# A two-layer decoder trunk on one core: plain order in the down stages, a split last tile, turned tiles behind whole pairs, and TensorE in written order

## The chip, the cores and the metric

The program runs on one core of a Trainium2 chip. The metric is the device time of one execution in microseconds (us), lower is better. Engines are named as in the profile: PE is TensorE (matmuls), PEld its weight loads, DVE is VectorE, ACT is ScalarE, POOL is GpSimd, SP issues DMAs.

## The reference

The program computes a decoder trunk of two layers on 256 tokens of width 1024, all in float32. `D_FF` is 2816, a head has 64 columns.

```python
def swiglu(x, w_gate, w_up, w_down):
    return (jax.nn.silu(x @ w_gate) * (x @ w_up)) @ w_down
...
    for layer in range(DEPTH):
        if layer == N_A_LAYERS:
            shared_kv = shared_moba_kv(h, positions, kv_norm_g, w_kv, k_norm_g)
        h = h + 0.5 * swiglu(rms_norm(h, ffn1_norm_g[layer]), ffn1_w_gate[layer], ...)
        hn = rms_norm(h, mix_norm_g[layer])
        if layer < N_A_LAYERS:      # convolution beside attention over a memory
            ...
        else:                       # block attention over the shared keys and values, beside the same
            ...
        h = h + jnp.concatenate([primary, mem_out], axis=-1) @ w_o[layer]
        h = h + 0.5 * swiglu(rms_norm(h, ffn2_norm_g[layer]), ffn2_w_gate[layer], ...)
```

The shared keys and values come from one projection of 1536 columns (768 keys, 768 values). The keys are normed by head and turned by position.

## The kernel before

The residual `x` lies in on-chip memory as eight tiles of 128 features by 256 tokens. A product of float32 is made from parts in the faster format that the kernel calls F32R: a weight is split into a rounded high part `wh` (a copy on ACT) and the rest `wl` (a subtraction on DVE), an input `y` into halves 0 (high) and 1 (low). Three products are summed: high by high, high by low, low by high.

All weights stream through the chip once, in chunks of which each half holds eight tiles of 128 by 128. `half_hi` (named `hi`, `lo` in the plan) makes `wh` and `wl` for such a half, with four buffers each.

**One FFN** is the function `ffn`; it runs four times, under the names a, b, c and d. For each of 22 blocks `j` it makes a gate tile `pg` and an up tile `pu`, each from eight input tiles `k`. `mm2` multiplies one weight tile: the high part against both halves of the input in one matmul of 512 columns (the sums land in the two halves of one PSUM bank), then the low part against the high input, 256 columns, into the lower half. The two together are called a pair here. After the last `k` the two halves are added. Trace names: `ag`, `au`, `ao` for the gate, up and down products of FFN a, and so for b, c, d; `ahs` for the activations.

The **down stage** of an FFN makes eight output tiles `m`, each from 22 tiles `k` of the activations. For the first seven, even `k` use `mm2` and odd `k` use `mm2_lo_first`, which puts the low part's matmul first, so two matmuls of 256 and two of 512 columns alternate. The last tile (`m` 7) uses `mm3`: three matmuls of 256 columns into one half of the bank, so that nothing has to be added from the other half. Its end is two DVE operations: `scalar_tensor_tensor` (scale) and `tensor_tensor` (add to `x`). The next stage's input tile is then split.

**Order.** Instructions go to the engines as a scheduler of the framework places them, by its own simulated timeline. The kernel can bind an engine: while a letter stands in `state["order"]`, `in_order` puts each instruction of that engine behind the last one written (P is TensorE, V, A and G are DVE, ACT and POOL). FFN a runs unbound. From layer 0's mixing the order is "P" or "PVA"; `ffn("b", ...)` clears it after its block 3; FFN c is unbound; layer 1's mixing is written out step by step (`MIX1`, "PVAG"), and FFN d is unbound again. `behind` puts one instruction after another without a semaphore.

**Small work inside a group.** A `plan` maps (block, gate or up, `k`) to a function that runs within `mm2`, between its two matmuls: `mean` (a norm's sums by matmuls of one column), `rows` (`bcast_rows`: two transposes that spread the norm over the partitions, PSUM tag `aux`), and turns. A turn is `to_heads_T`: two transposes of a token tile into a PSUM tile and one ACT copy out of it. In FFN b both turns of the memory keys follow the `rows` transposes at (3, g, 3); in FFN c both turns of the third key block come at (2, g, 4).

**Shared keys and values.** Between FFN b and FFN c, `proj` runs three times (`kv0`, `kv1`, `kv2`): 48 matmuls of 512 columns each, into two PSUM tiles by token block (tag `mm`, four buffers). `kv0` makes key blocks `sk0` and `sk1`, `kv1` makes `sk2` and the first values, `kv2` the other values. A key block of one token tile is copied out by ACT into a token tile (`sk0t`, tag `tok`, two buffers), normed and rotated on DVE and POOL, and turned (`sk0p`, tag `aux`, two buffers, shared with `bcast_rows`). `sk0` and `sk1` are turned without a written place. The norm `rkv` is written ahead of `kv0`.

Of the kernel before, what the change touches and what calls it, by code (L numbers as in the profile page):

```python
# [9 lines left out]
F32 = mybir.dt.float32  # L10
# [65 lines left out]
e5.a e6.x lo18 e6.h hi19 e7.x e6.l e6.q e7.h lo19 e6.a e7.q e7.a e7.l  # L76
""".split()
AHEAD = 3

POOL_NORM = (1,)  # L80

# [12 lines left out]
V_FFN1, V_MIX, V_MEM, V_FFN2, V_KV = 0, 16, 32, 48, 64  # L94
# [7 lines left out]
G_MQ, G_MK, G_K, G_Q = 0, 1, 3, 4  # L102
# [7 lines left out]
def tile_kernel(ctx: ExitStack, tc: tile.TileContext, w, xT, memT, pos, vec, hg, const, spec, out):  # L110
# [4 lines left out]
    tp = ctx.enter_context(tc.tile_pool(name="tp", bufs=2))  # L115
# [7 lines left out]
    x = cp.tile([P, KD, SEQ], F32, name="x")  # L123
# [26 lines left out]
    nc.vector.memset(mhalf, -0.5)  # L150


    state = {"chunk": 0, "half": 0, "raw": None, "order": "", "last": {}, "between": None, "made": []}

    class Ordered:

# [36 lines left out]
    def mmul(*a, **k):  # L193
        return in_order("P", nc.tensor.matmul(*a, **k))  # L194
# [57 lines left out]
    def mm3(o, wt, y, k, first, last, **kw):  # L252
        h, l = wt
        i = mmul(o, h, y[:, k, 0], start=first, stop=False, **kw)
        mmul(o, h, y[:, k, 1], start=False, stop=False, **kw)
        mmul(o, l, y[:, k, 0], start=False, stop=last, **kw)
        return i

    def mm2(o, wt, y, k, first, last, turn=None):

        h, l = wt
        a = mmul(o, h, y[:, k].rearrange("p a s -> p (a s)"), start=first, stop=False)
        if turn is not None:
            state["between"] = a
            turn()
            last_turn, state["between"] = state["between"], None
        b = mmul(o[:, :SEQ], l, y[:, k, 0], start=False, stop=last)
        if turn is not None:
            behind(b, last_turn)

    def mm2_lo_first(o, wt, y, k, last):
        h, l = wt
        mmul(o[:, :SEQ], l, y[:, k, 0], start=False, stop=False)
        mmul(o, h, y[:, k].rearrange("p a s -> p (a s)"), start=False, stop=last)

    def mm_group2(o, y, turns):
        for k, wt in enumerate(tiles_of(1)):
# [10 lines left out]
    def mm3_tok(o, wh, wl, y, t, k, c, first, last):  # L288
        s = slice(t * P, (t + 1) * P)
        mmul(o, y[:, k, 0, s], wh[:, c], start=first, stop=False)  # L290
        mmul(o, y[:, k, 0, s], wl[:, c], start=False, stop=False)
        mmul(o, y[:, k, 1, s], wh[:, c], start=False, stop=last)
# [33 lines left out]
        state["stat"] = state["last"]["P"]  # L326
        return v

    def rstd_cols(name, acc):
        v = mean_cols(name, acc)  # L330
        r = tp.tile([P, NT], F32, name=name, tag="rc", bufs=3)
        gps.tensor_tensor(r, v, mhalf[:, :NT], op=ALU.pow)
        return r

# [16 lines left out]
        return tp.tile([P, SEQ], F32, name=name, tag="acc")  # L351

    def ffn(name, y, acc, nexts, store=False, quick=False, hook=None, after=None, hook_down=None, r=None, plan=None,
            early=None, turns=()):


        plan = plan or {}
# [9 lines left out]

        def rows():
            norm["rb"] = bcast_rows(name + "nb", norm["r"])
            for turn in turns:  # L370
                turn()
# [15 lines left out]
        for j in range(KF):  # L387
# [27 lines left out]
            else:  # L415
# [10 lines left out]
                else:  # L426
                    mm_group2(pg, y, planned(j, "g"))
                    mm_group2(pu, y, planned(j, "u"))
            if early and j == 3:
                state["order"] = ""  # L430
            if j == 0 and "mean" not in plan.values() and r is None:
                mean()
            if rb is None and j < rows_at[0]:
# [19 lines left out]
        for m in range(KD):  # L453
            po = psum(f"{name}o{m}")
            if hook_down:
                with tc.issue_after(state["act"].ins):
                    hook_down(m)

            both_sums = m < KD - 1
            for k in range(KF):  # L460
                if both_sums and k % 2:
                    mm2_lo_first(po, next(it), hs, k, k == KF - 1)
                elif both_sums:
                    mm2(po, next(it), hs, k, k == 0, False)
                else:
                    mm3(po[:, :SEQ], next(it), hs, k, k == 0, k == KF - 1)
            if both_sums:
                d = both_halves(f"{name}d{m}", po, "g")
                dve.scalar_tensor_tensor(d, d, 0.5, rb, op0=ALU.mult, op1=ALU.mult)
            else:  # L470
                d = tp.tile([P, SEQ], F32, name=f"{name}d{m}", tag="g")
                dve.scalar_tensor_tensor(d, po[:, :SEQ], 0.5, rb, op0=ALU.mult, op1=ALU.mult)
            dve.tensor_tensor(x[:, m], d, x[:, m], op=ALU.add)
# [45 lines left out]
    def proj(name, y, *uses):  # L519

        os_ = [psum(f"{name}{t}") for t in range(NT)]
        n = MW * len(uses)
        per = HC // n
        for k0 in range(0, KD, per):
            wh, wl = half_chunk()
            for t in range(NT):
                for i in range(per):
                    k = k0 + i
                    mm3_tok(os_[t][:, :n], wh, wl, y, t, k, slice(i * n, (i + 1) * n), k == 0, k == KD - 1)
        for t in range(NT):  # L530
            for i, use in enumerate(uses):
                use(t, os_[t][:, i * MW:(i + 1) * MW])
# [152 lines left out]
    kv0 = []  # L685
# [456 lines left out]
    def sum_squares():  # L1142
# [7 lines left out]
        for t, tt in found:  # L1150
            key1.normed(t, tt)
        state["order"] = "P"

    (ykv, y), acc = ffn("b", y, acc, (V_KV, V_FFN1 + KD), plan={(2, "u", 1): "mean", (3, "g", 3): "rows"},
                        early=sum_squares, turns=mem_turns)


    rkv = rstd_cols("rkv", acc)
    turns = []
# [471 lines left out]
```

## Time and profile before

| | us |
|---|---|
| median of 3 runs | 962.6 |
| lowest and highest run | 961.28, 963.98 |
| the profiled execution, its own time | 963.06 |
| span from its first to its last instruction | 961.3 |

The profiled execution is 0.46 us above the median, and 1.8 us of its time lie outside its span. Views used below: the page's part 1 (busy time of each engine, its share of the span, its instructions); part 4 (the chain of work that ended last, shares by engine); the waits (who waited for whom: total us, times, longest); the chain in order of time (start, length, what, how many); and the timeline (start, length, engine, line, operation, tiles, shapes, count; idle time before it and what ended that in brackets). Matmul rows last longer than their distance, because matmuls are pipelined; the text therefore goes by starts. A transpose is a PE row of 128 columns.

### The profile page before, as it was taken

Reading aid. Unit: us, or ns where it says so; the run is one execution under the profiler, and the core shown is the slowest. Engines: PE = TensorE matmul, PEld = TensorE weight load, DVE = VectorE, ACT = ScalarE, POOL = GpSimd, SP = SyncE. Lnnn points to the kernel's source line nnn. Section 1 sums busy time; section 2 is a strip of 40 time slices with the busy share of each in tenths; the row PEclk is TensorE's granted clock in tenths of the full one; section 3 lists DMA queues with packets and bytes.
Section 4 is the critical chain, followed back from the end, with each engine's and each line's share of the span. In section 5 each row is a group of like instructions: output and inputs, shape, how many; then the busy total and the mean of one; then the engine's idle time right before and its main releaser. Section 6 shows DMA issues by size and latency. Waiting matters only on the chain.

```text
span 961.3 us, 15012 instructions
## 1 busy us (share of the span) xinstructions
PE 953.0 (99%) x5670; PEld 832.1 (87%) x5670; DVE 721.9 (75%) x1263; ACT 575.1 (60%) x1057; POOL 90.0 (9%) x89
## 2 busy tenths in 40 slices
PE   8999999999999999999999999999999999999998
PEld 6888888897888888888988888888897998888887
DVE  6898777776889877767767777767779578777663
ACT  6676566556686655655556665555548666556442
POOL 0122000110012000000123000000134120000000
PEclk9999999999999999999999999999999999999999
DMA  8755455454346555555555555555552245555550
GB/s 293 289 200 188 176 194 200 176 176 152 111 137 222 187 200 175 193 201 176 185 196 189 176 184 208 179 181 205 183 177 74 103 175 182 207 181 182 208 203 21
DMA packets 26569, 174.11 MB, mean 181 GB/s; under 512 B 3329, under 2 KB 4865, under 8 KB 6145
## 3 DMA queue, kind: packets, MB, share of 16 engines
q1 hardware_dynamic: 26208, 172.99, 50.5%
q8 instruction: 44, 0.72, 0.3%
q10 hardware_dynamic: 288, 0.17, 0.1%
q14 instruction: 29, 0.23, 0.1%
HBM read 172.10 MB, written 1.05 MB: 180 GB/s over the span
## 4 chain that ended last, share of the span: by engine, by line
PE 93%; DVE 4%; DMA 1%; ACT 1%; issue 0%; POOL 0%; SPq 0%
PE cg L194 8%; PE do L194 6%; PE ao L194 6%; PE co L194 6%; PE bo L194 6%; PE bu L194 6%; PE dg L194 6%; PE cu L194 6%; PE du L194 6%; PE bg L194 6%; PE ag L194 6%; PE au L194 6%; PE kv L194 3%; PE obo L194 2%; PE mkv L194 2%; DVE room L164 2%
## 5 line engine op out<-in xcount | busy, mean ns | idle before, releaser
L164 DVE TENSOR_TENSOR wl<-raw,wh 128x1024 fp32r<-128x1024 f32 (+1 forms) x326 | 395.8, 1216 | 168.7 <-ACT wh L164 166.8
L164 ACT ACTIVATE wh<-raw 128x1024 fp32r<-128x1024 f32 (+1 forms) x326 | 341.1, 1050 | 296.1 <-PE dg L194 27.1
L194 PE MATMUL ag<-y,wh 128*128 128x512 f32 x176 | 63.7, 398 | 0.5 <-ACT wh L164 0.5
L194 PE MATMUL au<-y,wh 128*128 128x512 f32 x176 | 63.4, 396 | 0.0
L194 PE MATMUL bg<-oay,wh 128*128 128x512 f32 x176 | 62.4, 393 | 0.1
L194 PE MATMUL dg<-oby,wh 128*128 128x512 f32 x176 | 62.5, 392 | 0.0
L194 PE MATMUL cu<-by,wh 128*128 128x512 f32 x176 | 62.3, 393 | 0.0
L194 PE MATMUL du<-oby,wh 128*128 128x512 f32 x176 | 62.3, 391 | 0.0
L194 PE MATMUL cg<-by,wh 128*128 128x512 f32 x176 | 62.2, 392 | 0.0
L194 PE MATMUL bu<-oay,wh 128*128 128x512 f32 x176 | 62.2, 392 | 0.0
L194 PE MATMUL bo<-bhs,wh 128*128 128x512 f32 (+1 forms) x198 | 55.8, 368 | 0.0
L194 PE MATMUL co<-chs,wh 128*128 128x512 f32 (+1 forms) x198 | 55.8, 368 | 0.0
L194 PE MATMUL do<-dhs,wh 128*128 128x512 f32 (+1 forms) x198 | 55.8, 368 | 0.0
L194 PE MATMUL ao<-ahs,wh 128*128 128x512 f32 (+1 forms) x198 | 55.8, 368 | 0.0
L194 PE MATMUL ag<-y,wl 128*128 128x256 f32 x176 | 48.9, 280 | 2.2 <-DVE wl L164 2.2
L194 PE MATMUL cg<-by,wl 128*128 128x256 f32 x176 | 49.4, 281 | 0.0
L194 PE MATMUL bg<-oay,wl 128*128 128x256 f32 x176 | 49.4, 281 | 0.0
L194 PE MATMUL bu<-oay,wl 128*128 128x256 f32 x176 | 49.4, 281 | 0.0
L194 PE MATMUL dg<-oby,wl 128*128 128x256 f32 x176 | 49.4, 280 | 0.0
L194 PE MATMUL cu<-by,wl 128*128 128x256 f32 x176 | 49.3, 280 | 0.0
L194 PE MATMUL du<-oby,wl 128*128 128x256 f32 x176 | 49.3, 280 | 0.0
L194 PE MATMUL au<-y,wl 128*128 128x256 f32 x176 | 48.7, 279 | 0.0
(960 smaller groups left out, 2242.9 us busy)
## 6 DMA issues: line engine op xcount, KB each, us to landing
raw<-in_w SPq DMA_DIRECT2D x158, 1024.0 KB, 4.8
raw<-in_w SPq DMA_DIRECT2D x5, 512.0 KB, 10.4
mT<-in_memT SPq DMA_DIRECT2D x1, 1024.0 KB, 8.4
out<-x SPq DMA_DIRECT2D x8, 128.0 KB, 1.7
dft<-in_spec SPq DMA_DIRECT2D x1, 817.0 KB, 10.2
raw<-in_w SPq DMA_DIRECT2D x2, 256.0 KB, 3.9
x<-in_xT SPq DMA_DIRECT2D x1, 512.0 KB, 8.8
x<-in_xT SPq DMA_DIRECT2D x2, 128.0 KB, 3.2
```

The source lines that it names most:

```text
L164: i = f(*a, **k)
L194: return in_order("P", nc.tensor.matmul(*a, **k))
```

## The change

The edit has four parts.

- **Down stages.** `mm2_lo_first` goes; tiles 0 to 6 use `mm2` for every `k`. Tile 7 uses `mm2` for `k` 0 to 13 (`APART` = 14), then `mm3` for `k` 14 to 21. After `k` 13 the upper half of its bank is scaled and added to `x` (`taken(po[:, SEQ:])`, two DVE operations), and after `k` 21 the lower half in the same way.
- **Small work behind whole pairs.** `mm2` runs its turn after both matmuls; the next pair's first matmul is put behind the turn's last transpose (`held`). The memory keys' two turns move from (3, g, 3) to (3, g, 4) and (3, g, 5), those of `sk2` from (2, g, 4) to (2, g, 6) and (3, g, 4).
- **TensorE in written order.** FFN b no longer clears the order after block 3; FFNs b, c and d set it to "P" after block 2.
- **Shared keys.** All key blocks are turned at written places: token tile 0 of `sk0` and `sk1` after `kv1`, token tile 1 of both after `kv2`, just ahead of FFN c's `bcast_rows`. The norm `rkv` is computed within `kv0`, behind its third weight half.

```diff
-    def mm2(o, wt, y, k, first, last, turn=None):
+    def mm2(o, wt, y, k, first, last, turn=None, closes=False, **kw):
         h, l = wt
-        a = mmul(o, h, y[:, k].rearrange("p a s -> p (a s)"), start=first, stop=False)
+        a = mmul(o, h, y[:, k].rearrange("p a s -> p (a s)"), start=first, stop=closes, **kw)
+        if state["held"] is not None:
+            behind(a, state["held"])
+            state["held"] = None
+        b = mmul(o[:, :SEQ], l, y[:, k, 0], start=False, stop=last, **kw)
         if turn is not None:
-            state["between"] = a
+            state["between"] = b
             turn()
-            last_turn, state["between"] = state["between"], None
-        b = mmul(o[:, :SEQ], l, y[:, k, 0], start=False, stop=last)
-        if turn is not None:
-            behind(b, last_turn)
-
-    def mm2_lo_first(o, wt, y, k, last):
...
+            state["held"], state["between"] = state["between"], None
...
-            if early and j == 3:
-                state["order"] = ""
+            if j == 2 and not first:
+                state["order"] = "P"
...
+            def taken(half):
+                d = tp.tile([P, SEQ], F32, name=f"{name}d{m}", tag="g")
+                dve.scalar_tensor_tensor(d, half, 0.5, rb, op0=ALU.mult, op1=ALU.mult)
+                dve.tensor_tensor(x[:, m], d, x[:, m], op=ALU.add)
+
             for k in range(KF):
-                if both_sums and k % 2:
-                    mm2_lo_first(po, next(it), hs, k, k == KF - 1)
-                elif both_sums:
-                    mm2(po, next(it), hs, k, k == 0, False)
+                if both_sums:
+                    mm2(po, next(it), hs, k, k == 0, k == KF - 1)
+                elif k < APART:
+                    mm2(po, next(it), hs, k, k == 0, False, closes=k == APART - 1, skip_group_check=True)
                 else:
-                    mm3(po[:, :SEQ], next(it), hs, k, k == 0, k == KF - 1)
+                    mm3(po[:, :SEQ], next(it), hs, k, False, k == KF - 1, skip_group_check=True)
+                if not both_sums and k == APART - 1:
+                    taken(po[:, SEQ:])
...
     def proj(name, y, *uses, within=None):
...
+            if within is not None and k0 == KD // 2:
+                within()
...
-    kuse = [keys(f"sk{i}", rkv, G_K, kTs, 2 * i, True, turns if i == 2 else None, 1) for i in range(3)]
+    kuse = [keys(f"sk{i}", rkv, G_K, kTs, 2 * i, True, turns[i], 1) for i in range(3)]
...
-    proj("kv0", ykv, kuse[0], kuse[1])
+    proj("kv0", ykv, kuse[0], kuse[1], within=lambda: rstd_cols("rkv", acc, rkv))
     proj("kv1", ykv, kuse[2], vuse[0])
+    turns[0][0]()
+    turns[1][0]()
     proj("kv2", ykv, vuse[1], vuse[2])
+    turns[0][1]()
+    turns[1][1]()
     (y,), acc = ffn("c", y, acc, (V_MIX + KD,), after=AF.Exp, r=rkv,
-                    plan={(2, "g", 4): lambda: [turn() for turn in turns]})
+                    plan={(2, "g", 6): turns[2][0], (3, "g", 4): turns[2][1]})
```

More of the change, by code (lines that the diff above doesn't have):

```diff
@@ L78 @@
 AHEAD = 3
+APART = 14
 POOL_NORM = (1,)
@@ L150, in tile_kernel @@
     nc.vector.memset(mhalf, -0.5)
-    state = {"chunk": 0, "half": 0, "raw": None, "order": "", "last": {}, "between": None, "made": []}
+    state = {"chunk": 0, "half": 0, "raw": None, "order": "", "last": {}, "between": None, "held": None, "made": []}
     class Ordered:
@@ L257, in mm3 @@
         return i
-    def mm2(o, wt, y, k, first, last, turn=None):
+    def mm2(o, wt, y, k, first, last, turn=None, closes=False, **kw):
         h, l = wt
-        a = mmul(o, h, y[:, k].rearrange("p a s -> p (a s)"), start=first, stop=False)
+        a = mmul(o, h, y[:, k].rearrange("p a s -> p (a s)"), start=first, stop=closes, **kw)
[3 more added lines that the diff above has]
+        b = mmul(o[:, :SEQ], l, y[:, k, 0], start=False, stop=last, **kw)
         if turn is not None:
-            state["between"] = a
+            state["between"] = b
             turn()
-            last_turn, state["between"] = state["between"], None
-        b = mmul(o[:, :SEQ], l, y[:, k, 0], start=False, stop=last)
-        if turn is not None:
-            behind(b, last_turn)
-    def mm2_lo_first(o, wt, y, k, last):
-        h, l = wt
-        mmul(o[:, :SEQ], l, y[:, k, 0], start=False, stop=False)
-        mmul(o, h, y[:, k].rearrange("p a s -> p (a s)"), start=False, stop=last)
+            state["held"], state["between"] = state["between"], None
     def mm_group2(o, y, turns):
@@ L327, in mean_cols, with rstd_cols @@
         return v
-    def rstd_cols(name, acc):
+    def rstd_cols(name, acc, r=None):
         v = mean_cols(name, acc)
-        r = tp.tile([P, NT], F32, name=name, tag="rc", bufs=3)
+        if r is None:
+            r = tp.tile([P, NT], F32, name=name, tag="rc", bufs=3)
         gps.tensor_tensor(r, v, mhalf[:, :NT], op=ALU.pow)
@@ L353, in ffn @@
     def ffn(name, y, acc, nexts, store=False, quick=False, hook=None, after=None, hook_down=None, r=None, plan=None,
-            early=None, turns=()):
+            early=None):
         plan = plan or {}
@@ L369, in rows @@
             norm["rb"] = bcast_rows(name + "nb", norm["r"])
-            for turn in turns:
-                turn()
         def planned(j, which):
@@ L469, in ffn @@
                 dve.scalar_tensor_tensor(d, d, 0.5, rb, op0=ALU.mult, op1=ALU.mult)
+                dve.tensor_tensor(x[:, m], d, x[:, m], op=ALU.add)
             else:
-                d = tp.tile([P, SEQ], F32, name=f"{name}d{m}", tag="g")
-                dve.scalar_tensor_tensor(d, po[:, :SEQ], 0.5, rb, op0=ALU.mult, op1=ALU.mult)
-            dve.tensor_tensor(x[:, m], d, x[:, m], op=ALU.add)
+                taken(po[:, :SEQ])
             if store:
@@ L517, in to_heads_T, with proj @@
                              pp[:, :2 * P].rearrange("p (a b) -> p a b", a=2), AF.Copy, scale=scale)
-    def proj(name, y, *uses):
+    def proj(name, y, *uses, within=None):
         os_ = [psum(f"{name}{t}") for t in range(NT)]
@@ L1152, in sum_squares @@
         state["order"] = "P"
[L1154 to L1159, printed above, removed]
-    kuse = [keys(f"sk{i}", rkv, G_K, kTs, 2 * i, True, turns if i == 2 else None, 1) for i in range(3)]
+    (ykv, y), acc = ffn("b", y, acc, (V_KV, V_FFN1 + KD), plan={(2, "u", 1): "mean", (3, "g", 3): "rows", (3, "g", 4): lambda: mem_turns[0](),
+                              (3, "g", 5): lambda: mem_turns[1]()},
+                        early=sum_squares)
+    rkv = tp.tile([P, NT], F32, name="rkv", tag="rc", bufs=3)
+    turns = [[] for _ in range(3)]
+    kuse = [keys(f"sk{i}", rkv, G_K, kTs, 2 * i, True, turns[i], 1) for i in range(3)]
     vuse = [values(f"sv{i}", rkv, vs, i * MW) for i in range(3)]
-    proj("kv0", ykv, kuse[0], kuse[1])
+    proj("kv0", ykv, kuse[0], kuse[1], within=lambda: rstd_cols("rkv", acc, rkv))
     proj("kv1", ykv, kuse[2], vuse[0])
+    turns[0][0]()
+    turns[1][0]()
     proj("kv2", ykv, vuse[1], vuse[2])
+    turns[0][1]()
+    turns[1][1]()
     (y,), acc = ffn("c", y, acc, (V_MIX + KD,), after=AF.Exp, r=rkv,
-                    plan={(2, "g", 4): lambda: [turn() for turn in turns]})
+                    plan={(2, "g", 6): turns[2][0], (3, "g", 4): turns[2][1]})
     qT = cp.tile([P, KD, SEQ], F32, name="q1T", tag="t8k")
```

## The prediction, made before the change was run

> **What bounds the kernel now.** I read the page's part 1 first, then its part 4, then TensorE's waits.
>
> ```profile
> PE 953.0 (99%) x5670; PEld 832.1 (87%) x5670; DVE 721.9 (75%) x1263; ACT 575.1 (60%) x1057; POOL 90.0 (9%) x89
> ...
> PE 93%; DVE 4%; DMA 1%; ACT 1%; issue 0%; POOL 0%; SPq 0%
> ```
>
> ```profile
> PE ag L194 <- DVE wl L164: 2.2, 1, 2.2
> PE pw L131 <- DVE onec L133: 1.4, 1, 1.4
> PE ag L194 <- ACT wh L164: 0.5, 2, 0.3
> PE a4pp L197 <- ACT room L164: 0.2, 1, 0.2
> ```
>
> TensorE is busy for 99% of the span and carries 93% of the chain. All its waits add up to 4.3 us, and all but 0.2 us of that lies in the start-up and FFN a, which the edit leaves alone there. So there is almost nothing to win from waits: a gain can only come from denser matmuls, and any wait that the edit puts in front of TensorE is paid in full.
>
> How dense the matmuls are comes from two views. First the chain in order of time, in FFN d:
>
> ```profile
> 790.71 2.77 PE dg L194 x16
> ...
> 893.33 2.77 PE du L194 x16
> 896.10 61.53 PE do L194 x374
> ```
>
> From 790.71 to 896.10 lie 38 groups of eight pairs in plain order: 105.39/304 = 346.7 ns a pair. Second the timeline of the same FFN's down stage:
>
> ```profile
> 895.94 0.39 PE L194 MATMUL do<-dhs,wh 128*128 128x512 f32 x1
> ...
> 949.39 0.63 PE L194 MATMUL do<-dhs,wh 128*128 128x512 f32 x3
> 949.87 0.28 PE L194 MATMUL do<-dhs,wl 128*128 128x256 f32 x1
> ...
> 957.34 0.28 PE L194 MATMUL do<-dhs,wl 128*128 128x256 f32 x1
> 957.65 0.42 DVE L164 SCALAR_TENSOR_TENSOR dd<-do,dnb 128x256 f32<-128x256 f32 x1 [6.07 <-PE do L194]
> ```
>
> From 895.94 to 949.39 go 153 pairs and one low matmul, in alternating order: (53.45 − 0.12)/153 = 348.6 ns a pair. From the first to the last low matmul of tile 7, 949.87 to 957.34, go 21 triples: 355.7 ns each. DVE starts 0.31 us after the last matmul's start and takes 0.42 us; both are used below.
>
> **Part by part.** The sum is made on the profiled execution (963.06 us, 0.46 us above the median of 962.6).
>
> *Plain order in tiles 0 to 6.* No instruction is added or removed. If the pairs run as in the gate stage, 154 × (348.6 − 346.7) = 0.29 us an FFN, 1.2 us in four. If the 1.9 ns come from another thing than the order, it is 0; I see no reason for a loss. I take −1.2, because the gate rows are the same matmuls in the very order that is written now.
>
> The Trainium skill ("TensorE: Matmul & The Clock Gate", section "Back-to-back issue gap") gives an isolated matmul N/2.4 + 2.5 ns, which is 325 ns a pair and the same in either order; by it this term would be an estimate of 0 and the whole sum 1.2 us higher. The trace has 346.7 and 348.6 ns, so the rule's level does not fit here and I go by the rows.
>
> *Pairs in tile 7.* 14 triples become pairs, 14 matmuls and their weight loads fewer: 14 × (355.7 − 346.7) = 0.13 us an FFN, −0.5 us in four. The eight triples left keep their price.
>
> *The early half of tile 7.* This adds two DVE operations beside TensorE. Their own time (0.42 us each) is covered, as DVE is only 75% busy. But the first reads the upper half of a PSUM bank whose lower half the next matmul writes. What happens then is shown where layer 1's mixing does the same: there `mqJ` holds two token blocks in one bank, ACT reads the first block, and TensorE then writes the second.
>
> ```profile
> 704.50 0.28 PE L194 MATMUL mqJ<-wh,cy 128*128 128x256 f32 x1
> ...
> 704.63 0.50 PE L194 MATMUL rqp<-onec,cacc 128*128 128x1 f32 x4
> 704.83 0.39 ACT L164 ACTIVATE room<-mqJ 128x256 f32<-128x256 f32 x1 [0.33 <-PE mqJ L194]
> 705.26 0.19 PEld L194 LDWEIGHTS mqJ<-wh,cy 128*128 128x128 f32 x1 [0.22 <-ACT room L164]
> 705.26 0.38 PE L194 MATMUL mqJ<-wh,cy 128*128 128x256 f32 x1
> ...
> 705.49 0.28 PE L194 MATMUL mqJ<-wl,cy 128*128 128x256 f32 x1
> ```
>
> The read runs from 704.83 to 705.21 (columns of the first block only); the weight load for the second block is released by that read, at 705.26. So the halves of a bank are not independent: TensorE waits until the reader is done, starts 0.05 us later, and its first matmul then takes 0.23 instead of 0.12 us. In tile 7 the same matmul order is bound, with nothing to put in between (FFN a is unbound, but the mixing's first matmul stands behind FFN a's last). Everything behind `k` 13 queues behind that wait: 24 matmuls, and through them the next stage.
>
> The Trainium skill says the same from the hardware's side ("PSUM — Partial Sum Buffer", section "PSUM bank collisions raise a hardware error"): accesses of two engines to one bank collide at disjoint columns too, so software must guard by bank. It speaks against the change, and the row above agrees with it.
>
> Without other work on DVE, counted from tile 7's start S: the last low matmul before the wait starts at 14 × 0.3467 − 0.12 = 4.73, DVE at 5.04, TensorE again at 5.04 + 0.42 + 0.05 = 5.51 instead of 4.85, and 0.11 us for the slow first matmul: 0.77 us. That is FFN d, where DVE has only tile 6's end. In a, b and c the splits of tile 6 stand at that very place:
>
> ```profile
> 202.85 0.96 DVE L164 SCALAR_TENSOR_TENSOR ay<-x,vt,ay 128x256 fp32r<-128x256 f32 x1
> ```
>
> ```profile
> 478.38 1.36 DVE L164 SCALAR_TENSOR_TENSOR by<-x,vt,by 128x256 fp32r<-128x256 f32 x2
> 480.07 1.23 DVE L164 TENSOR_TENSOR wl<-raw,wh 128x1024 fp32r<-128x1024 f32 x1 [0.33 <-ACT wh L164]
> ```
>
> ```profile
> 697.01 0.96 DVE L164 SCALAR_TENSOR_TENSOR cy<-x,vt,cy 128x256 fp32r<-128x256 f32 x1
> ```
>
> Tile 7 starts 53.69 us after the stage (949.39 + 0.24 − 895.94). The stages start here:
>
> ```profile
> 144.63 0.39 PE L194 MATMUL ao<-ahs,wh 128*128 128x512 f32 x1
> ```
>
> ```profile
> 420.18 0.39 PE L194 MATMUL bo<-bhs,wh 128*128 128x512 f32 x1
> ```
>
> ```profile
> 638.80 0.39 PE L194 MATMUL co<-chs,wh 128*128 128x512 f32 x1
> ```
>
> So S is 198.32, 473.87 and 692.49. DVE comes free at S + 5.49 (a), S + 5.87 (b) and S + 5.48 (c); with 0.03 to start, 0.42, 0.05, 0.11 and less 4.85 that makes 1.25, 1.63 and 1.24 us. Sum over four: +4.9 us. Ends: four times the bare 0.77, +3.1, if DVE takes the early half first; and 1.23 us more in three FFNs, +8.6, if a weight copy like the one at 480.07 is placed ahead of it. I take 4.9, the order in which things become ready in these rows.
>
> *Transposes behind whole pairs.* The counts stay. A pair with two transposes in it:
>
> ```profile
> 786.16 0.39 PE L194 MATMUL dg<-oby,wh 128*128 128x512 f32 x1
> 786.39 0.38 PE L197 MATMUL dnbp<-cst,dnr 128*128 128x128 f32 x2
> 786.53 0.36 PE L194 MATMUL dg<-oby,wl 128*128 128x256 f32 x1
> 786.73 0.40 PE L194 MATMUL dg<-oby,wh 128*128 128x512 f32 x1
> ```
>
> It takes 0.57 instead of 0.35 us, 0.11 us a transpose, which is about the distance of two transposes; breaking the pair costs nothing beyond that. Moving them: 0. In FFN c the turns need `sk2` some 15 us after `kv2`, which is ample.
>
> *Written order.* In the trace no wait of TensorE lies in b, c, d or the key stretch, so there is nothing to win. There is one place to lose. Ahead of FFN c the written order is two transposes of `sk0`, two of `sk1`, two of `bcast_rows`: three tiles on the two buffers of `aux`, so the third must wait for ACT's copy out of the first, with FFN c's first matmul behind it. Before, the scheduler had spread them:
>
> ```profile
> 514.45 0.38 PE L197 MATMUL sk0p<-cst,sk0t 128*128 128x128 f32 x2
> ```
>
> ```profile
> 515.61 0.38 PE L197 MATMUL sk1p<-cst,sk1t 128*128 128x128 f32 x2
> ...
> 518.65 0.38 PE L197 MATMUL cnbp<-cst,rkv 128*128 128x128 f32 x2
> ```
>
> ```profile
> 514.93 0.48 ACT L164 ACTIVATE kvs<-sk0p,vt 128x256 f32<-128x256 f32 x1
> 515.29 0.48 ACT L164 ACTIVATE sk2t<-kv,rkv 128x256 f32<-128x256 f32 x1
> 515.64 1.22 ACT L164 ACTIVATE kvs<-kv,rkv 128x256 f32<-128x256 f32 x3
> ...
> 517.02 1.10 ACT L164 ACTIVATE wh<-raw 128x1024 fp32r<-128x1024 f32 x1
> 517.97 0.52 ACT L164 ACTIVATE kvs<-sk1p,vt 128x256 f32<-128x256 f32 x1
> ```
>
> From a turn to its copy went 0.48 us for one and 2.36 us for the other, since ACT was full. Adding 0.48 for the copy and 0.05, less the 0.44 us of the four transposes, TensorE would wait 0.6 to 2.4 us; I take the middle, 1.5, since here too value copies and a weight copy come due on ACT just then. Earlier, `sk0` and `sk1` of token tile 1 can only be copied out when the turns of tile 0 have freed their two token buffers, and `kv2`'s second tile waits for the PSUM that they hold: a race within a few tenths, 0 to 1.1 us (one ACT weight copy); I take 0.3. The norm inside `kv0` costs the same matmuls at another place: 0. Key stretch: +1.8, ends 0.6 and 3.5.
>
> **Sum:** −1.2 − 0.5 + 4.9 + 0 + 1.8 = +5.0 us. On the median: 967.6 us, 0.5% slower.
>
> **The rivals.**
> - *Not slower: the halves of tile 7's bank are independent.* If the matmul of `k` 14 needn't wait for the read of other columns, the 4.9 us go and the sum is +0.1: 962.7 us; with a free key stretch −1.7: 960.9. The `mqJ` rows speak against it. It decides as soon as the four waits together stay under 2.8 us (then the sum is under 0.3%).
> - *Waits at their bare size.* DVE takes the early half first (3.1) and ACT copies `sk0p` at once (0.6): −1.7 + 3.7 = +2.0, 964.6 us. Against it: DVE's splits in a, b and c are due before the early half is.
> - *A weight copy ahead of the early half* in a, b and c: +3.7 on the forecast, 971.3 us. Against it: in b the copy waits for ACT until 480.04, after the early half is due.
>
> **How the numbers follow.** Under about 0.3% (2.9 us) a measurement of this kernel can't be told from no change: 959.7 to 965.5 is "same". Forecast 0.55, weight copies ahead 0.13, bare waits 0.19, independent halves 0.10, something outside this list that helps 0.03. The forecast's own ends (plain order worth 0, key stretch 0.6 to 3.5) span 966.4 to 970.5. The range must take in bare waits and most of the weight-copy case: 963.5 to 971.5. Slower: 0.55 + 0.13 = 0.68; same 0.28; faster 0.04.
>
> **What would show it.** The waits of TensorE list `ao`, `bo`, `co`, `do` released by DVE, 0.6 to 1.6 us each; the same before `cnbp`, released by ACT. The chain has down stages whose first seven tiles take 53.4 instead of 53.7 us. The prediction is wrong if those waits are missing, if DVE's early half starts before the splits of tile 6, or if plain pairs in the down stage take other than 346.7 ns.

## The result, and the profile after

The changed kernel takes 972.82 us (median; 971.48 to 974.75) against 962.37 for the kernel before on the same chip: ratio 1.0109 [1.0083, 1.0135], 10.4 us slower. The forecast was 967.6 us, so it had the direction and a little under half of the size; the time lies above its range. The profiled execution takes 971.59 us.

The page's parts 1 and 4 of the changed kernel:

```profile
PE 956.9 (99%) x5614; PEld 832.8 (86%) x5614; DVE 726.0 (75%) x1271; ACT 575.1 (59%) x1057; POOL 88.3 (9%) x89
...
PE 91%; DVE 5%; ACT 1%; DMA 1%; issue 1%; POOL 0%; SPq 0%; ACTq 0%
```

TensorE has 56 matmuls fewer and is busy 3.9 us longer: so some of the loss is not waiting but slower matmuls. The rest is in its waits:

```profile
PE cnbp L198 <- ACT kvs L165: 2.5, 1, 2.5
...
PE bo L195 <- DVE bd L165: 1.2, 1, 1.2
PE co L195 <- DVE cd L165: 0.8, 1, 0.8
PE ao L195 <- DVE ad L165: 0.8, 1, 0.8
...
PE do L195 <- DVE dd L165: 0.6, 1, 0.6
PE kv L195 <- ACT sk1t L165: 0.4, 1, 0.4
```

These six are new and make 6.3 us. All of the kinds that the prediction named are there, the one ahead of `cnbp` longer than forecast. The chain in order of time (start, length, what, how many) tells how dense the matmuls are:

```profile
317.41 2.77 PE bu L195 x16
...
417.25 2.77 PE bu L195 x16
...
520.63 0.43 PE cnbp L198 x2
521.06 3.60 PE cg L195 x14
524.66 2.84 PE cu L195 x14
...
528.19 2.77 PE cg L195 x16
...
903.64 58.98 PE do L195 x336
...
963.22 3.09 PE do L195 x24
```

From 317.41 to 417.25 lie 36 groups of eight pairs: 346.7 ns a pair, as in the gates of before. But the down stage's 168 plain pairs take 58.98/168 = 351.1 ns, and the first groups of FFN c (3.60 us for seven pairs) are far slower than those behind them.

By stage, from the start of one to the start of the next, in us:

| | before | after | difference |
|---|---|---|---|
| down stages a, b, c, d | 61.53, 61.52, 61.52, 61.52 | 62.89, 63.29, 62.92, 62.65 | +5.66 |
| of these, tile 7 | 7.83 each | 8.84, 9.24, 8.85, 8.60 | +4.20 |
| `kv0` to the start of FFN c's gates | 34.05 | 37.66 | +3.62 |
| gates of c | 123.06 | 124.14 | +1.08 |
| everything else behind 145 us | | | −0.23 |

That is +10.1 us. The stretch up to the first down stage, in which the edit moves only the norm's few small matmuls, was 1.6 us shorter in this execution (143.0 for 144.6; it lies between 142.6 and 146.0 in all profiled executions here), so the two profiled executions differ by 8.5.

### The profile page after: what moved, and what is told of

The parts are those of the page before. It is cut to its first block, busy times and chain, and to the rows that moved or that the text cites. A ratio compares the mean times of both kernels' runs of the same rounds, so it can differ in the third digit from the quotient of the medians.

```text
span 969.8 us, 14952 instructions
## 1 busy us (share of the span) xinstructions
PE 956.9 (99%) x5614; PEld 832.8 (86%) x5614; DVE 726.0 (75%) x1271; ACT 575.1 (59%) x1057; POOL 88.3 (9%) x89
## 3 DMA queue, kind: packets, MB, share of 16 engines
HBM read 172.10 MB, written 1.05 MB: 179 GB/s over the span
## 4 chain that ended last, share of the span: by engine, by line
PE 91%; DVE 5%; ACT 1%; DMA 1%; issue 1%; POOL 0%; SPq 0%; ACTq 0%
PE cg L195 8%; PE do L195 6%; PE cu L195 6%; PE bu L195 6%; PE dg L195 6%; PE du L195 6%; PE bg L195 6%; PE co L195 6%; PE bo L195 6%; PE ao L195 6%; PE ag L195 6%; PE au L195 6%; PE kv L195 3%; PE obo L195 2%; PE mkv L195 2%; DVE room L165 2%
## 5 line engine op out<-in xcount | busy, mean ns | idle before, releaser
L195 PE MATMUL bo<-bhs,wh 128*128 128x512 f32 (+1 forms) x184 | 62.0, 384 | 1.2 <-DVE bd L165 1.2
L195 PE MATMUL co<-chs,wh 128*128 128x512 f32 (+1 forms) x184 | 62.0, 384 | 0.8 <-DVE cd L165 0.8
L195 PE MATMUL ao<-ahs,wh 128*128 128x512 f32 (+1 forms) x184 | 61.9, 384 | 0.8 <-DVE ad L165 0.8
L195 PE MATMUL do<-dhs,wh 128*128 128x512 f32 (+1 forms) x184 | 62.0, 384 | 0.6 <-DVE dd L165 0.6
L195 PE MATMUL co<-chs,wl 128*128 128x256 f32 x176 | 49.9, 283 | 0.0
L195 PE MATMUL bo<-bhs,wl 128*128 128x256 f32 x176 | 49.9, 283 | 0.0
L195 PE MATMUL do<-dhs,wl 128*128 128x256 f32 x176 | 49.9, 283 | 0.0
L195 PE MATMUL ao<-ahs,wl 128*128 128x256 f32 x176 | 49.7, 283 | 0.0
```

## The experiments

Four questions: do tile 7's waits come from the shared bank; does the key stretch wait for a PSUM buffer, and what do the slow pairs behind it come from; why do plain pairs not take 346.7 ns; and do the moved turns cost anything.

**Own bank for the end of tile 7** (from the changed kernel):

```diff
-                    mm3(po[:, :SEQ], next(it), hs, k, False, k == KF - 1, skip_group_check=True)
+                    if k == APART:
+                        rest = psum(f"{name}p{m}")
+                    mm3(rest[:, :SEQ], next(it), hs, k, k == APART, k == KF - 1)
```

Both halves of `po` are taken after `k` 13, `rest` after `k` 21.

> The changed kernel, but tile 7's last eight k go to a PSUM tile of their own, so that DVE's early read and TensorE's next matmul meet in different banks (two DVE operations more per FFN). Theory (the waits in tile 7 are the shared bank): no wait of TensorE on DVE in ao, bo, co, do; tile 7 takes 14 x 351.3 + 8 x 355.7 = 7.76 us in each FFN instead of 8.84, 9.24, 8.85 and 8.6; about 4.5 us less than the changed kernel, 968.3 us. Rival (DVE is simply late, or holds something else that the matmuls need): waits of about 1 us stay, 972 to 973 us.

Measured: 969.98 us, 1.0074 [1.0054, 1.0094]. The waits of `ao`, `bo`, `co`, `do` are gone, and tile 7 takes 7.80, 7.76, 7.80 and 7.76 us: 4.4 us less than in the changed kernel. The timeline of FFN b shows TensorE passing where it stood for 1.24 us before:

```profile
479.55 0.29 PE L195 MATMUL bo<-bhs,wl 128*128 128x256 f32 x1
...
479.68 0.40 PE L195 MATMUL bp<-bhs,wh 128*128 128x256 f32 x2
...
480.53 0.74 DVE L165 SCALAR_TENSOR_TENSOR bd<-bo,bnb 128x256 f32<-128x256 f32 x2
```

DVE reads the old bank 0.85 us after TensorE has gone on in the new one. DVE is as late as before and TensorE no longer waits, so meeting in one tile and one bank is shown to be the cause. The edit gives the end a tile and a bank of its own at once; whether the program's wait goes by the tile or by the bank, it does not tell. The time fell by only 2.8 us; in the profile FFN c's gates ran slow (125.86 us for 124.14), which is the last question.

**Own tag for the early transposes**: FFN c's `bcast_rows` takes its PSUM tile from `sc`, which is idle there, and not from `aux`.

```diff
-        pb = psum(name + "p", "aux", 2)
+        pb = psum(name + "p", "sc" if name == "cnb" else "aux", 2)
```

> The changed kernel, but FFN c's row transposes take a PSUM tile of the tag sc instead of the third of aux. Theory (the wait ahead of them is for ACT's copy out of the first of two buffers, and the half clock behind it comes from TensorE's idle time): the wait of 2.5 us goes, the granted clock stays at 1.0 through FFN c's first blocks, and 2.7 + 1.5 = 4.2 us go: 968.6 us. Rival (the clock falls there for another reason, as the load after a stretch of wide matmuls): only 2.7 us go, 970.1 us, and a stretch of about 3.4 us at half clock stays.

Measured: 971.88 us, 1.0097 [1.0075, 1.0119]. The wait ahead of `cnbp` is gone, the stretch takes 34.92 us instead of 37.66, and the first 14 pairs of FFN c run at full speed. So the wait is for the third tile on two buffers, as predicted. The time hardly moved; c's gates took 124.55 us in the profile, more than with the wait, at the slower of two paces that are told of below.

**The wait filled**: 11 matmuls on constants stand in TensorE's order between the turns and `cnbp`, so that it is busy while it would wait.

```diff
+    pf = psum("fill", "sc", 2)
+    for i in range(11):
+        mmul(pf, busy[:, :P], busy, start=True, stop=True)
     (y,), acc = ffn("c", ...
```

> The changed kernel with eleven matmuls of 512 columns in the 16-bit format, whose results nobody reads, put between the last turn and FFN c's row transposes: about 2.4 us of TensorE work inside a wait of 2.7 us. Theory (idle time halves the clock): the wait for ACT stays where it is, but TensorE is busy through it; no half clock behind it, 1.5 us less: 971.3 us. Rival (the clock falls for another reason): the half clock stays, 972.8 us or more.

Measured: 972.29 us, 1.0097 [1.0077, 1.0116]; the key stretch is as long as before the filling (37.71 us), c's gates are 122.82 instead of 124.14, while those of b, far ahead of the edit, took 125.80 instead of 123.76 in this execution and hide the gain. Windows of this kernel, of the changed one and of the one with its own tag (length, busy time and count of PE, PEld, DVE, ACT, POOL, then TensorE's granted clock, DMA share, GB/s):

```profile
518.00:520.60 2.60, 0.10 (x1) 0.00 (x0) 1.08 (x1) 2.60 (x7) 0.00 (x0) 1.00 0.44 186
520.60:523.00 2.40, 2.37 (x12) 2.05 (x13) 1.52 (x6) 1.68 (x5) 0.03 (x1) 0.79 0.37 116
523.00:526.00 3.00, 3.00 (x13) 2.62 (x12) 1.44 (x4) 0.00 (x0) 2.65 (x3) 0.60 0.63 262
```

(the changed kernel);

```profile
520.60:523.00 2.40, 2.24 (x13) 0.98 (x11) 1.23 (x1) 2.40 (x7) 0.00 (x0) 1.00 0.30 119
523.00:526.00 3.00, 3.00 (x19) 2.62 (x18) 1.37 (x5) 1.36 (x5) 0.94 (x1) 1.00 0.63 213
```

(filled);

```profile
523.00:526.00 3.00, 3.00 (x19) 2.65 (x18) 1.38 (x5) 1.85 (x5) 1.54 (x2) 1.00 0.86 314
```

(own tag). A further changed kernel, the one with `hs` at another place (below), has the same wait of 2.53 us, unfilled, ahead of `cnbp` at 524.13. Its window right behind it:

```profile
524.10:526.50 2.40, 2.37 (x14) 2.09 (x15) 1.52 (x6) 1.69 (x5) 0.02 (x1) 1.00 0.48 113
```

In the changed kernel TensorE is idle from 518.1 on, and from 521.9, 1.3 us after it has resumed, its pairs start 640 ns apart for about 3.4 us, at half the clock; 13 matmuls start in a window that elsewhere holds 19. Where the same wait is filled with work, or isn't there, the clock stays at 1.00. The mean granted clocks of the timed executions agree: 0.998 in all four of the changed kernel, 0.999 or 1.000 in all four of the filled one.

But the drop doesn't come each time. Five profiles have the wait unfilled; in four of them a stretch of 3.41 us at half clock follows, which begins between 0.2 us ahead of `cnbp` and 1.3 us behind it, and in the fifth the clock stayed at 1.00 and c's gates took 122.82 us, as with the wait filled. So idleness can lower the clock here, and when it does, the price behind a 2.5 us wait is another 1.3 us (124.14 against 122.82); what decides whether it does stays open. The Trainium skill ("TensorE: Matmul & The Clock Gate", section "What's actually happening") has a window of 3413 ns for this gate, after which an idle engine falls to half its clock; the length of the slow stretch agrees, but 2.53 us of idleness were enough here in four profiles of five.

**Alternating down tiles**: the changed kernel with `mm2_lo_first` at odd `k` of tiles 0 to 6 again.

> The changed kernel with the alternating order of before in the down stages' tiles 0 to 6. Theory (the order of the two widths sets the pair's time in this stage): a pair goes from 351.3 back to 348.5 ns, 0.43 us an FFN, 1.7 us in all: 971.1 us. Rival (something else in the changed kernel slows the pairs, such as the bound order or other DVE and ACT work beside them): 351 ns stay, 972.8 us.

**The kernel before with plain order alone**:

```diff
-                if both_sums and k % 2:
-                    mm2_lo_first(po, next(it), hs, k, k == KF - 1)
-                elif both_sums:
-                    mm2(po, next(it), hs, k, k == 0, False)
+                if both_sums:
+                    mm2(po, next(it), hs, k, k == 0, k == KF - 1)
```

> The kernel before with only the plain order in the down stages' tiles 0 to 6. Theory (the order of the widths alone): 351.0 ns a pair, +1.5 us over the kernel before, hardly measurable. Rival (the bound order or the new tile 7 slows the pairs): 346.7 to 348.6 ns, 0 to -1.2 us.

Measured: 973.06 us, 1.0099 [1.0072, 1.0126] for the first (its start took 145.6 us in its profile, 2.6 more than the changed kernel's, and c's gates 126.1); 963.34 us, 1.0015 [1.0006, 1.0024] for the second. By stage they agree with each other: the pairs of tiles 0 to 6 take 348.5 ns in alternating and 351.0 in plain order. FFN d's down stage in the chain, plain in the second, where the prediction showed 61.53 for the alternating one:

```profile
895.52 62.00 PE do L194 x374
```

**`hs` at another place**: the changed kernel, with the activations in a pool of their own at higher addresses.

```diff
-        hs = cp.tile([P, KF, 2, SEQ], F32R, name=name + "hs", tag="hs")
+        hs = hp.tile([P, KF, 2, SEQ], F32R, name=name + "hs", tag="hs")
...
```

The tiles `hc` and `room`, which share the buffer of `hs`, move with it.

> The changed kernel with the activations of the down stages moved from low addresses of the on-chip memory to high ones, above the weights and the inputs; nothing else. Theory (plain pairs take 351 instead of 346.7 ns because of where their moving operand lies): the down stages' pairs go to 346.7 ns, about 2.6 us less. Rival (place does not matter; the down stage falls into the slower of two paces that the gate stages show too, 346.7 and 353.3 ns): 351 ns stay.

Measured: 972.32 us in one execution. The down pairs are no longer 351.0 ns in all FFNs but 352.1 in a, 353.3 in b, 346.7 in c and in d. In b, c and d the gates just ahead ran at these very paces (353.3, 346.7 and 346.7). In a the gates ended at 346.7, and so the down stage began; from the 26th pair on it ran at 353.2. There, in the unbound FFN a, the matmuls of two neighbouring pairs stand in swapped order (timeline of TensorE):

```profile
152.49 0.62 PE L196 MATMUL ao<-ahs,wh 128*128 128x512 f32 x2
152.95 0.40 PE L196 MATMUL ao<-ahs,wl 128*128 128x256 f32 x2
```

The same swap with the same change of pace stands in the last kernel below. The chain of FFN d:

```profile
905.12 58.25 PE do L196 x336
```

58.25/168 = 346.7 ns, for 351.1 in the changed kernel. Only places in memory were changed, so plain order isn't slow as such: where its operands lie decides. Taking `hs` out of its pool may also move what lies above it, so that it is the place of `hs` alone is argued: the weights pass through the same buffers in the gates, and these kept their two paces.

**All three repairs together** (own bank, own tag, alternating):

> The changed kernel with all three repairs: tile 7's last eight k in a bank of their own, FFN c's row transposes on the tag sc, alternating order in tiles 0 to 6. What stays of the change are pairs in tile 7, turns behind whole pairs and the bound order. Theory (the slowdown is the shared bank 4.5, the wait with the clock behind it 4.2, the order of widths 1.6 us): within 0.1% of the kernel before, +0.3 us (-0.3 for tile 7, +0.6 for the wait in kv2 that stays). Rival (binding TensorE's order costs by itself): 2 us or more above the kernel before.

Measured: 965.34 us (962.59 to 967.57), 1.0033 [1.0023, 1.0043]. The down stages take 61.45, 61.43, 61.42 and 61.41 us, the key stretch 34.94. About 3 us over before remain. 0.9 of them are the key stretch; behind it c's gates took 124.55 us in the profile, for 123.06 before, and in the gates what is left of the change is the place of the turns and TensorE's written order.

**Where the turns stand.** The gates of b, c and d run at one of two paces, 346.7 or 353.3 ns a pair, in plain order at the same clock, and keep a pace until something interrupts the row of pairs. The profile of before shows such a change (chain, FFN b):

```profile
308.15 2.83 PE bg L194 x16
...
314.25 1.30 PE bg L194 x7
315.55 0.22 PE bnbp L197 x2
315.77 0.44 PE mk1p L197 x4
316.21 1.52 PE bg L194 x9
317.73 2.77 PE bu L194 x16
```

The groups take 2.83 us ahead of the transposes and 2.77 behind them; FFN c does the same at its turns. A second execution of the changed kernel, unchanged, was to show how much hangs on it:

> The changed kernel once more, unchanged, to see what in the traces repeats. Theory (a stretch of plain pairs settles on one of two paces by chance, at each interruption): waits in tile 7 and ahead of FFN c repeat to within 0.1 us and the down stages take 351 ns again, but one gate stage or another may run at 353.3 instead of 346.7 ns, worth about 2 us each. Rival (the pace is a property of the program): FFN b, c and d's gate stages take 346.7 ns again.

It took 975.83 us, 4.2 more than the first, with the same waits in tile 7 and ahead of `cnbp`. Its gates of b and c took 125.76 and 126.39 us instead of 123.76 and 124.14. The chain in FFN b:

```profile
317.45 2.83 PE bu L195 x16
...
419.21 2.83 PE bu L195 x16
```

36 groups in 101.76 us are 353.3 ns a pair, with the clock at 1.00. So two kernels tested the turns' place alone. First the repaired kernel with turns inside pairs again:

```diff
         a = mmul(o, h, ...)
-        if state["held"] is not None:
-            behind(a, state["held"])
-            state["held"] = None
+        if turn is not None:
+            state["between"] = a
+            turn()
+            last_turn, state["between"] = state["between"], None
         b = mmul(o[:, :SEQ], l, ...)
-        if turn is not None:
-            state["between"] = b
-            turn()
-            state["held"], state["between"] = state["between"], None
+        if turn is not None:
+            behind(b, last_turn)
```

> The kernel with all three repairs (own bank in tile 7, own tag for the early transposes, alternating down tiles), and the turned tiles again inside the pairs of the gates, so that TensorE resumes after them with a low matmul of 256 columns. Theory (the pace of the pairs holds until TensorE is interrupted, and a resumption with the low matmul sets the fast one): the gates of b and c run at 346.7 ns a pair for most of their length in every execution, as in before (123.8 and 123.1 us); the time is about 2.0 us below the 965.3 of the repaired kernel with turns behind whole pairs: 963.3, its runs within 961.5 to 964.5. Rival (the pace is set by chance at the start of a layer, and where the turns stand doesn't matter): 965.3 as before, runs spread over 962.6 to 967.6, with gates at 353.3 ns in some traces.

Then the kernel before with the opposite edit and nothing else:

> The kernel before with one part of the change alone: the turned tiles stand behind whole pairs, and TensorE resumes with the high matmul of 512 columns. Nothing else differs. Theory (such a resumption leaves a slow pace as it is): the gates of b and of c, which begin at 353.3 ns a pair in the profile of before, keep that pace in many executions, for up to 2 us each: median 963.5 to 966, with a spread of runs of 3 to 5 us. Rival of the prediction (where the turn stands costs nothing): 962, with the spread of before (961 to 964).

Measured: 962.72 us (960.64 to 966.20), 1.0006 [0.9996, 1.0016], against 1.0033 for the same kernel with turns behind whole pairs; and 963.83 us (961.07 to 967.61), 1.0019 [1.0005, 1.0032], against 1 for the same kernel with turns inside. So the place of the turns costs about 2 us in both, by the timed runs, and as the first of the two kept the written order, that order isn't what costs. Nor is it the clock: with the executions at a mean granted clock of 0.998 or less left out, the 21 of the kernel before lie at 960.95 to 962.44 us, and of the nine of its edited twin four lie at 965.70 to 966.20. The profiled executions at hand showed no difference (c slow in both of the first pair, b and c fast in both of the second), so four more were taken, of the two kernels unchanged.

> The repaired kernel with turns inside the pairs once more, unchanged (median 962.7, but 966.2 in its profiled execution, with the gates of c at 353.3 ns and 146.0 us up to the first down stage). Theory (the pace changes from execution to execution, and turns inside pairs make the fast one the more frequent): an execution of 961 to 963 with c at 346.7 ns, some 122.6 us for its gates. Rival (c is always slow with the early transposes on their own tag): c at 124.5 us again, the difference in the start alone.

> The repaired kernel with turns inside pairs a third time, unchanged. Theory: the gates of c at 122.6 us in an execution of 961 to 963. Rival: 124.5 us.

> The kernel before with turns behind whole pairs once more, unchanged (median 963.8, runs 961.1 to 967.6; its profiled execution of 962.1 had b and c fast). Theory: in executions of 963.5 and more b or c (or both) at 353.3 ns, 125.4 and 125.0 us for their gates instead of 123.8 and 123.1. Rival (the spread is the start's alone): b and c as in before, 143 to 146 us up to the first down stage.

> The kernel before with turns behind whole pairs a third time, unchanged. Theory: b or c at 353.3 ns where the execution takes 963.5 us or more. Rival: the start alone differs.

The first two took 965.62 and 966.11 us, both with c at 124.56 us and a late start (145.4 and 145.9): here the rival was right, and no profile of this kernel shows c fast. The late starts have a cause of their own in part: between 10 and 17 us the mean granted clock is 0.76 in both, as in four other profiles here (first down stage at 144.8 to 146.0 us in these six), and 1.00 in the fourteen others (142.6 to 145.6). That its runs of 960.6 to 961.7 had c fast is argued from their time alone: its profiled executions, with their starts put at 143 us, would come to about 963.2. The other two took 967.15 and 962.14 us. The chain of the slower one in FFN b:

```profile
317.94 2.82 PE bu L194 x16
...
419.70 2.82 PE bu L194 x16
```

and of the first execution of this kernel (962.14 us as well):

```profile
316.97 2.77 PE bu L194 x16
...
416.81 2.77 PE bu L194 x16
```

101.76 against 99.84 us for 36 groups; c went with it (125.08 against 123.06 us). Together 3.9 of the 5.0 us between the two, the rest is the start (144.9 against 143.9). So behind whole pairs the slow pace can hold through both stages, as the theory says, in one profile of three; the three kernels that are before but for the down stages and have the turns inside (before itself, plain order alone, and the last one below) have b and c at the fast pace behind the turns in their profiles, one each. With turns inside and c slow in three profiles of the repaired kernel, the traces alone don't tell the two places apart; the timed runs do.

My theory also had a rule for it: that a resumption with the matmul of 256 columns sets the fast pace. It was put to a direct test, with many cuts by two transposes of a constant, in a repeating order of one inside a pair (resumed with 256 columns) and two ahead of a pair (512):

> The repaired kernel with turns inside pairs, and two further transposes of a constant in nearly every group of eight pairs of the gates of b, c and d (from the fourth tile on), by turns inside a pair, so that TensorE resumes with the low matmul of 256 columns, and twice ahead of a pair, so that it resumes with the high one of 512. The time is longer by these transposes and is not compared; what counts is the pace of the pairs ahead of and behind each of some 110 cuts. Theory (a resumption with the low matmul sets the fast pace, one with the high matmul may leave or bring the slow one): behind a low resumption 346.7 ns nearly always, whatever stood ahead; slow stretches begin only behind high resumptions and last over the next of them. Rival (each interruption draws the pace anew by chance): slow stretches as often behind the one as behind the other. Second rival (the pace hangs on the layer's operands): whole layers at one pace, whatever the cuts.

Measured: 988.1 us, and the opposite. Behind the cuts inside a pair (with the few of the kernel's own) 35 of 38 fast stretches went slow (353.8 ns), behind those ahead of a pair 71 of 76 stretches were fast. The rule has fallen. So has the first rival: the pattern repeats with hardly an exception, which isn't chance. If the pace is set by the cut, it must be possible to choose it; two cuts in block 6 of b, c and d, one in its gate and one in its up group, the second ahead of a pair in one kernel and inside it in its twin:

> The repaired kernel with turns inside pairs (962.7), and in the seventh gate tile of b, c and d two cuts of two transposes each, both ahead of a pair of k 5. From the run with many cuts: behind a second such cut the pairs ran at 346.7 ns nearly always. Theory (the pace of a stage is set where TensorE resumes, holds to the end of the stage, and is what the time follows): the groups from the eighth tile on at 2.77 us in b, c and d in its profile; c 1.7 us shorter than the 124.5 us that it had in the three profiles with the same early transposes, less what two cuts cost (0.2 to 0.25 us each, in b and d too). Against its twin with a low cut: about 5 us less. Rival (the pace is of the stage, whatever the cuts; or it moves no end): the same time as the twin within 0.5 us.

> The twin: the same six cuts, but the second of each stage stands inside the pair of k 5, so that TensorE resumes with the low matmul. In the run with many cuts 35 of 43 such cuts led to 353.8 ns. Theory: b, c and d at 353.3 ns from the eighth tile on, 15 tiles of 16 pairs by about 6.9 ns, 1.7 us a stage, 5 us in all above the twin: some 967 to 969. The gates of d, which ran at 346.7 ns in every profile so far, show it best. Rival: the same time as the twin within 0.5 us.

Measured: 965.20 us, 1.0036 [1.0026, 1.0046], and 968.36 us, 1.0062 [1.0048, 1.0076]. The chain in FFN d, which runs fast in every profile without added cuts, first with the high cut, then with the low:

```profile
814.82 2.77 PE dg L195 x16
...
892.47 2.77 PE dg L195 x16
```

```profile
817.62 2.82 PE dg L195 x16
...
891.11 2.83 PE dg L195 x16
```

28 groups in 77.65 us (346.7 ns a pair) against 26 in 73.49 (353.3). The gates of d took 127.67 and 129.28 us, those of b 124.27 and 125.93. In c the two changed places: 124.76 with the high cut, 123.15 with the low. That leaves 1.7 us net in the profiles where 5 were expected, and 3.2 between the medians. So, as far as one profile of each shows, a cut sets the pace of all that follows in the stage, 1.6 to 1.7 us here, and the same cut in one place sets the other pace in another. What the cut must meet for the fast one stays open; the size of the matmul behind it alone is not it.

**The best of the parts**: the kernel before, with plain order, `hs` at the higher place, and tile 7 with pairs for 14 `k` and its own bank for the rest; turns inside pairs.

> The kernel before with the down stages in plain order, the hidden values in a pool of their own at high addresses (where the down pairs took the gates' own pace, 346.7 or 353.3 ns, and not 351.0), and the seventh down tile with pairs for its first 14 k and a PSUM tile of its own for the rest. Turns inside pairs as in before. Theory: where the gates end at 346.7 ns, the 126 down pairs of that layer follow at 346.7 for 348.6, 0.24 us less each, and the seventh tile is 0.07 less each: together about 1.2 us, 960.8. Rival (the down stage takes its own pace, 351 to 353 ns): 0.3 to 0.6 us more for each layer, 963 to 964.5.

Measured: 961.05 us (960.40 to 963.16), 0.9992 [0.9983, 1.0002], not distinguishable from before. The chain has what was expected from FFN b on:

```profile
896.13 58.25 PE do L195 x336
```

The down stages of b, c and d take 61.12 us instead of 61.52. In a the pairs ran at 352.1 ns, with the change of pace shown above, and the stage took 62.06, which gives nearly half of it back.

## Why the prediction was right in direction and short in size

*Pairs and the early half of tile 7 (−0.5 and +4.9, net +4.4).* Right. Measured +4.2 by stage. The waits are 4.4 of it against a bank of its own (1.04, 1.48, 1.05 and 0.84 us in a to d, put at 1.25, 1.63, 1.24 and 0.77), and the pairs give 0.2 (put at 0.5, but these pairs ran at 351 ns too). The order on DVE was the forecast one in all three, as the timeline of the changed kernel shows for FFN b:

```profile
478.40 1.35 DVE L165 SCALAR_TENSOR_TENSOR by<-x,vt,by 128x256 fp32r<-128x256 f32 x2
...
479.67 0.41 DVE L165 SCALAR_TENSOR_TENSOR bd<-bo,bnb 128x256 f32<-128x256 f32 x1
...
480.12 0.43 DVE L165 TENSOR_TENSOR x<-bd,x 128x256 f32<-128x256 f32 x1
...
480.23 0.48 PE L195 MATMUL bo<-bhs,wh 128*128 128x256 f32 x2 [1.24 <-DVE bd L165]
```

The early half starts when the splits are through, and TensorE 0.15 us after its end (0.05 in the row of `mqJ`). FFN d, where nothing stood ahead on DVE, paid about the bare price. The rivals "halves independent" and "a weight copy ahead" are out.

*Plain order (−1.2).* Wrong: +1.5. The failed step is "I take −1.2, because the gate rows are the same matmuls in the very order that is written now": the order was the same, but not the place of the moving operand. In the down stage plain pairs took 351.0 ns with `hs` at its old place and 346.7 to 353.3 with it at another. No row of before had plain pairs on `hs`, so the honest bounds were 0 to −1.2 and the same on the other side; "I see no reason for a loss" closed that side without a row.

*Written order in the key stretch (+1.8, ends 0.6 and 3.5).* Right in place and mechanism, too small: +4.7 with what lies behind it. Its parts are three. The wait ahead of `cnbp` was put at 1.5, the middle of 0.6 and 2.4, and is 2.5. The timeline of the changed kernel shows why:

```profile
517.50 0.38 PE L198 MATMUL sk0p<-cst,sk0t 128*128 128x128 f32 x2
...
517.70 0.84 ACT L165 ACTIVATE kvs<-kv,rkv 128x256 f32<-128x256 f32 x2 [0.53 <-PE kv L195]
...
518.43 1.05 ACT L165 ACTIVATE wh<-raw 128x1024 fp32r<-128x1024 f32 x1
519.38 0.47 ACT L165 ACTIVATE sk2t<-kv,rkv 128x256 f32<-128x256 f32 x1
...
519.73 0.48 ACT L165 ACTIVATE kvs<-kv,rkv 128x256 f32<-128x256 f32 x1
520.09 0.49 ACT L165 ACTIVATE kvs<-sk0p,vt 128x256 f32<-128x256 f32 x1
```

The copy that frees the buffer comes sixth on ACT, behind three copies of `kvs`, a weight copy and one of `sk2t`: exactly what the row of 2.36 us had shown for `sk1p`. The text named that cause ("since here too value copies and a weight copy come due") and then halved it. The races for buffers earlier in the stretch cost 0.4 to 0.6 (put at 0.3). And 1.3 us were in no term: the halved clock behind the wait. That leaves 0.3 to 0.5 us unassigned.

*Transposes behind whole pairs (0).* Wrong: about 2 us in the timed runs, from nothing to 4 in one execution. The step "breaking the pair costs nothing beyond that. Moving them: 0" priced the transposes themselves, which is right, but not the pairs behind them; the trace of before had rows of 2.83 and 2.77 us on either side of a turn, which the term leaves out. What sets the pace stays open.

By size: +10.1 us by stage against +5.0 predicted is 2.7 for the plain order, 2.9 for the key stretch, less 0.2 for tile 7 and 0.2 for everything else. The turns come on top in some executions: the two profiled ones of the changed kernel, 971.59 and 975.83, stand on either side of the median. This part of the ledger doesn't close to a microsecond, since the paces and the start change from one execution to the next.

## What to carry to other kernels

Where TensorE is the bound, price not only what an edit adds to its queue but the state that it leaves behind: a wait that leaves it idle can cost half as much again in halved clock, in some executions and not in others, and interruptions of a dense stream can decide the pace of hundreds of matmuls behind them. A duration from another stage, where an operand lies elsewhere, is a bound and not a value. When two engines meet in one PSUM bank at different columns, count the wait in full, or give the second half its own bank.

## What the runs showed of the hardware

- Plain pairs of the gates run at two paces at the same granted clock of 1.00, 346.7 and 353.3 ns (2.77 and 2.83 us for eight). A pace holds for 100 us and more. In b, c and d it changed only where other work broke the row of pairs; in a's down stage with `hs` at the higher place it changed where two matmuls stood in swapped order, with no idle time. The same program shows both paces in different executions, and cuts by two transposes can set either.
- On `hs` at its old place neither occurs: 351.0 ns in plain and 348.5 in alternating order, whatever the gates had; at the higher place the down pairs of b, c and d take the gates' pace.
- An idle stretch of 2.53 us was followed by 3.41 us at half of TensorE's clock in four profiles of five, beginning between 0.2 us before work resumed and 1.3 us after; in the fifth, and with the stretch filled with matmuls, the clock stayed at 1.00.
